# The adaLN sums of the first layer's gate and of the second layer's shift and scale: from beside the gates into slots of the memory stage, by blocks of 128 columns

## The chip, the cores and the metric

The kernel runs on one core of a Trainium2 chip. Its time is the device time of one execution in microseconds; less is better. The engines that matter here are TensorE (PE, with its weight loads, PEld), VectorE (DVE), ScalarE (ACT), GpSimd (POOL) and SyncE (SP), which issues nearly all DMAs. Each engine works through its own instructions in the order in which the program has them, and waits for the others by semaphores.

## The reference, cut to what matters

One inference step of a two-layer diffusion backbone, in fp32: 1024 latent tokens ("sample") and 256 context tokens ("prompt") of width 1024. Layer 0 has two groups of heads from one projection, a windowed attention (A) and a bidirectional mLSTM matrix memory (B, 4 heads of 256 x 256 state, two directions); layer 1 is a latent attention (C). In front of each layer the normed input is scaled and shifted, and behind each the output is gated, by rows that a small product makes from the conditioning (adaLN):

```python
def _adaln(cond, w, b):
    m = jax.nn.silu(cond) @ w + b
    shift, scale, gate = jnp.split(m[:, None, :], 3, axis=-1)
    return shift, scale, gate
...
        sh_p, sc_p, gt_p = _adaln(c_ctx[None, :], w_mod[l], b_mod[l])
        sh_s, sc_s, gt_s = _adaln(c, w_mod[l], b_mod[l])
        hp = _rmsnorm(yp, norm_g[l]) * (1.0 + sc_p) + sh_p
        hs = _rmsnorm(ys, norm_g[l]) * (1.0 + sc_s) + sh_s
        ...
            out_p, (k_ctx, v_ctx, mem, nrm_, mx) = _mixer_ab(hp, *wts, None, None)
        ...
        yp = yp + gt_p * out_p
        ys = ys + gt_s * out_s
```

`w_mod[l]` is 1024 x 3072 in fp32, and there are two conditionings, one of the samples and one of the prompt. The change concerns three of the six 1024-column parts of the two layers: the gate of layer 0, and the shift and scale of layer 1.

## The kernel before, in words

TensorE's time goes to products of fp32 values, each made of three passes over two rounded halves (`wh`, `wl` of the weights, `hTh`, `hTl` of the tokens). The weights of a projection come in blocks of 256 columns (`DenseBlock`): a DMA brings two of the eight row tiles at a time (`wf`), ScalarE rounds each to `wh` (L353), POOL subtracts to get `wl` (L354), TensorE runs the block's units (for each of three chunks of tokens and two halves of columns, 24 matmuls), and a function of the block's own evacuates each unit.

The stages, with their times in the trace of the kernel before: start, norms and first values (0 to 60 us); the block of attention values with the gates' 16 columns (60 to 90.4); four blocks of the memory's head 0, namely queries (QB), keys (KB), values (VB) and output gate (OB), beside the scalar gates of the memory (90.4 to 240); the memory stage (240 to 1098); the attention stage (1098 to 1500); the output projection of layer 0 (1500 to about 1600); layer C (to the end, at 2643).

The adaLN sums are not made on TensorE as a product: `mod_steps` (L284) makes them by blocks of 512 columns. For each of eight row tiles a DMA brings 128 x 512 of `w_mod` (`mw`, 256 KB), and VectorE multiplies it with the conditioning's column (L319 for the first tile) or multiplies and adds (L321) into `macc`, one operation for each of the two conditionings. `total` then sums over the partitions with two fp32 matmuls against a selecting matrix (`sel`, in the trace under the tile name `unit`), takes a bank from `K.ps()`, adds the bias (`bmod`, L306), and stores the row in DRAM (`modd`). Six such blocks, 2 of layer 0's gate and 4 of layer 1's shift and scale, are due here: 96 operations on VectorE, 48 DMAs of `mw`. (The shift and scale of layer 0 are made earlier, the gate of layer 1 later, near 1660 to 1790 us by 256 columns; neither is touched.)

What sets the order before 240 us: `layer_ab` calls `dense.run(1, 1)`, a weave of `gates(...)` with `dense.stream(1, 1)`, and `dense.run(3, 1)`; the stream takes one step of `dense.mods` (two VectorE operations) for every unit of cost that a projection block spends. What is left of the sums is drained, and `mod_cols(K, 1, mp)` fetches layer 1's rows and turns them into columns. A scheduler then places the instructions on each engine. `gates` makes the log gates, transposes them to rows (`LI`, `LF`), scans them along the tokens (`gB` sums, `gM` running maxima, L1328 to L1335), and transposes the results back to columns, `K.cols`: ten transposes of each of three 36-row tiles.

In the memory stage the order is written by hand (`manual_schedule`). `beside_memory` goes through 174 slots: in each, the steps of the visits that are due (a visit is one chunk of 128 tokens, one head, one direction; 80 of them, two slots apart), what earlier slots put off by `K.later`, a share of the units of 24 projection blocks, and `dense.pump`, which asks for weights and splits them. PSUM there has three banks S for the visits, three `mm` for projection units, and two T for transposes.

## Time and profile before

| what | value |
|---|---|
| median of 3 runs | 2644.18 us (2643.71 to 2646.58) |
| profiled execution: its own time | 2644.84 us |
| profiled execution: span | 2643.0 us |
| TensorE busy | 2572.9 us (97%) |
| VectorE busy | 1777.3 us (67%) |
| ScalarE busy | 1406.5 us (53%) |
| POOL busy | 1167.1 us (44%) |
| DMA | 348.79 MB, mean 132 GB/s |

The busy shares are averages over all stages. A wait counts where the engine that waits is the one that sets the stage's end; that is read from the stage. The ends of matmuls are modelled, since they are pipelined: the distance between two starts is the measure of what one takes.

### The profile page before, as it was taken

What the parts mean: (1) busy time and instruction counts of PE and PEld (TensorE: products, weight loads), DVE (VectorE), ACT (ScalarE), POOL (GpSimd) and SP (SyncE); (2) the same over time, 40 slices, a digit from 0 to 9 for tenths busy, and PEclk for the clock granted to TensorE, in tenths of its full rate; (3) what the DMA queues carried; (4) which work ended last, traced back from release to release, by engine and by line L of the source; (5) the groups of instructions that cost most, each with busy time, mean ns of one, the idle gap of its engine ahead of it and who ended that gap; (6) DMA issues with size and microseconds to landing.
All of it is one profiled execution on the core that took longest, in us unless ns stands there. A gap on an engine that the chain in (4) does not pass through costs nothing.

```text
span 2643.0 us, 48201 instructions
## 1 busy us (share of the span) xinstructions
PE 2572.9 (97%) x16209; PEld 2262.3 (86%) x16209; DVE 1777.3 (67%) x4040; ACT 1406.5 (53%) x3598; POOL 1167.1 (44%) x1533
## 2 busy tenths in 40 slices
PE   7989999999999999989999999999899999999998
PEld 6878899898998888868888877987799999999887
DVE  6883565655746666388777545335788888888853
ACT  5222443543533433287666533322788888888842
POOL 4342333423434434275545453223455545555642
PEclk9989999999999999999999999999999999999999
DMA  7554556556657655463433463333311101101333
GB/s 247 181 157 157 161 178 198 175 171 195 199 169 225 213 164 185 140 204 111 136 102 111 130 197 130 121 95 114 104 30 30 44 29 40 35 19 30 122 104 128
DMA packets 344586, 348.79 MB, mean 132 GB/s; under 512 B 29610, under 2 KB 291415, under 8 KB 344083
## 3 DMA queue, kind: packets, MB, share of 16 engines
q1 hardware_dynamic: 344338, 345.71, 42.1%
q8 instruction: 129, 2.11, 0.3%
q14 instruction: 119, 0.97, 0.1%
HBM read 235.09 MB, written 110.51 MB: 131 GB/s over the span
## 4 chain that ended last, share of the span: by engine, by line
PE 81%; DVE 6%; DMA 3%; ACT 3%; issue 3%; POOL 2%; SPq 1%; POOLq 0%; DVEq 0%; ACTq 0%
PE mm L103 34%; PE S L103 27%; PE V L103 8%; PE T L107 6%; PE D L103 3%; PE mm L107 2%; SPq L138 1%; PE T L103 1%; DVE macc L321 1%; DVE att_nm L1109 0%; DVE xT L536 0%; ACT att_p L1114 0%; POOL wl L354 0%; DMA o_x<-y 0%; DMA w<-in_w_out_ab 0%
## 5 line engine op out<-in xcount | busy, mean ns | idle before, releaser
L354 POOL TENSOR_TENSOR wl<-wf,wh 128x256 fp32r<-128x256 f32 (+2 forms) x288 | 250.7, 896 | 448.6 <-ACT wh L353 378.6
L103 PE MATMUL mm<-hTh,wh 128*128 128x512 f32 (+1 forms) x912 | 328.6, 360 | 1.6 <-DVE scr L620 0.9
L103 PE MATMUL mm<-hTl,wh 128*128 128x512 f32 (+1 forms) x912 | 325.5, 357 | 0.0
L103 PE MATMUL mm<-hTh,wl 128*128 128x512 f32 (+1 forms) x912 | 325.4, 357 | 0.0
L103 PE MATMUL S<-cK,cQ 96*128 96x512 f32 (+3 forms) x1248 | 298.3, 364 | 3.3 <-ACT cPb L2154 1.0
L2202 DVE TENSOR_TENSOR cpl<-T,cph 128x512 fp32r<-128x512 f32 x336 | 228.5, 685 | 38.0 <-ACT cph L2201 34.5
L103 PEld LDWEIGHTS S<-cK,cQ 96*128 96x128 f32 (+1 forms) x1248 | 192.8, 189 | 25.9 <-ACT cPb L2154 2.9
L2201 ACT CAST cph<-T 128x512 fp32r<-128x512 f32 x336 | 192.3, 589 | 26.6 <-PE T L107 13.4
L103 PEld LDWEIGHTS mm<-hTh,wl 128*128 128x128 f32 x912 | 172.0, 189 | 26.4
L103 PEld LDWEIGHTS mm<-hTh,wh 128*128 128x128 f32 x912 | 171.9, 188 | 25.7 <-DVE bmod L306 1.7
L103 PEld LDWEIGHTS mm<-hTl,wh 128*128 128x128 f32 x912 | 171.9, 188 | 22.9
L2152 DVE TENSOR_REDUCE cmx<-S 128x1 f32<-128x512 f32 x256 | 172.7, 681 | 16.4 <-PE S L103 15.2
L103 PE MATMUL V<-cph,cV 128*128 128x256 f32 x672 | 177.0, 290 | 1.0 <-DVE co L2217 1.0
L103 PE MATMUL V<-cpl,cV 128*128 128x256 f32 x672 | 171.9, 285 | 1.3 <-DVE cpl L2202 1.3
L103 PE MATMUL S<-w,o_ah 128*128 128x512 f32 x492 | 152.1, 395 | 3.0 <-ACT w L819 1.9
L103 PE MATMUL mm<-w,o_ah 128*128 128x512 f32 x468 | 151.4, 402 | 0.0
L2133 POOL TENSOR_SCALAR cPa<-cPa,cst 128x512 f32<-128x512 f32 x128 | 99.3, 776 | 118.0 <-DVE cst L2130 87.5
L1123 POOL TENSOR_SCALAR att_p<-att_p,att_den 128x640 f32<-128x640 f32 (+1 forms) x128 | 97.5, 774 | 103.4 <-DVE att_den L1120 41.0
L1134 ACT CAST att_ph<-mm 128x512 fp32r<-128x512 f32 x168 | 98.5, 586 | 81.5 <-PE mm L107 80.0
L353 ACT CAST wh<-wf 128x256 fp32r<-128x256 f32 (+2 forms) x288 | 102.0, 409 | 70.1 <-DMA wf<-in_w_in_ab 30.5
L1135 DVE TENSOR_TENSOR att_pl<-mm,att_ph 128x512 fp32r<-128x512 f32 x168 | 115.7, 689 | 32.1 <-ACT att_ph L1134 27.3
L103 PE MATMUL mm<-wh,hTh 128*128 128x256 f32 x480 | 135.8, 283 | 0.0
(432 smaller groups left out, 7823.5 us busy)
## 6 DMA issues: line engine op xcount, KB each, us to landing
wf<-in_w_in_ab SPq DMA_DIRECT2D x120, 256.0 KB
in<-in SPq DMA_DIRECT2D x40, 514.0 KB
in<-in SPq DMA_DIRECT2D x32, 386.0 KB
mw<-in_w_mod SPq DMA_DIRECT2D x48, 256.0 KB
in<-scr SPq DMA_DIRECT2D x40, 258.0 KB
o_x<-y SPq DMA_DIRECT2D x20, 512.0 KB
wm<-in_w_mod SPq DMA_DIRECT2D x16, 512.0 KB
in<-cx SPq DMA_DIRECT2D x32, 256.0 KB
```

The lines of the kernel that those rows point to most:

```text
L103: return self.nc.tensor.matmul(out, lhsT, rhs, start=start, stop=stop)
L107: self.nc.tensor.transpose(out, in_, self.ident[:p, :p])
L138: self.nc.sync.dma_start(f(out), f(in_))
L353: K.nc.scalar.copy(wh, wf[:, k])
L354: K.nc.gpsimd.tensor_sub(wl, wf[:, k], wh.bitcast(F32))
L1123: nc.gpsimd.tensor_scalar(pv, pv, den[:, i:i + 1], 1.0, ALU.mult, ALU.mult)
L1134: K.nc.scalar.copy(ph, self.T)
L1135: K.nc.vector.tensor_sub(pl, self.T, ph.bitcast(F32))
L2133: nc.gpsimd.tensor_scalar(pv, pv, wt[:, c:c + 1], rd, ALU.mult, ALU.mult)
L2152: nc.vector.tensor_reduce(mx[:, b, c:c + 1], S, AX.X, ALU.max, negate=True)
L2201: nc.scalar.copy(ph, T_)
L2202: nc.vector.tensor_sub(pl, T_, ph.bitcast(F32))
```

## The change

The six blocks of 512 columns become 24 of 128. `mod_slots` replaces `mod_steps` for them: a DMA brings two row tiles of 128 columns (128 KB, in pieces of 512 bytes, two buffers), one step makes four VectorE operations of 128 columns (two at L364 and two at L366, or four at L366), and behind the eighth row tile the total's two matmuls, now 128 columns wide, the bias (L352) and the store follow, each put off by a slot. There are 96 steps. They are taken in the loop over slots of the memory stage, in those slots two behind which a block is `light`; a slot adds 4 x 24 / (0.52 x 174) = 1.06 steps when it is. Not light are the attention's query blocks and the memory's query and key blocks; all others are. The total takes its bank from the three `mm` banks.

`mod_cols` for layer 1 moves behind the attention stage, ahead of the loads of the output weights. `K.cols` becomes three tiles of 8 columns a chunk instead of 36, filled by two copies each, and the visits' column numbers follow.

```diff
@@ -331,2 +331,48 @@
 
+def mod_slots(K, p, blocks):
+
+    nc = K.nc
+    parts = [(l, f, k) for l, f in blocks for k in range(0, KD, 2)]
+    asked = []
+
+    def ask():
+        if parts:
+            l, f, k = parts.pop(0)
+            w = K.t(p, [128, 2, 128], F32, "mw", 2)
+            K.dma(w, K.I["w_mod"][l, k * 128:(k + 2) * 128, f:f + 128].rearrange("(k p) f -> p k f", p=128))
+            asked.append(w)
+
+    def total(l, f, acc, bm):
+        ps = K.ps()
+        for cd in range(2):
+            K.mm(ps[0:2, 0:128], K.sel[cd], acc[:, cd], cd == 0, cd == 1)
+        K.later(partial(out, l, f, bm, ps))
+
+    def out(l, f, bm, ps):
+        nc.vector.scalar_tensor_tensor(bm, ps[0:2, 0:128], 0.5, bm, ALU.mult, ALU.add)
+        K.later(lambda: K.dma(K.modd[l][:, f:f + 128], bm))
+
+    for _ in range(2):
+        ask()
+    for l, f in blocks:
+        acc = K.t(p, [128, 2, 128], F32, "macc", 1)
+        for k in range(KD):
+            w = asked[0][:, k % 2, :]
+            for cd in range(2):
+                c = K.condT[:, cd * KD + k:cd * KD + k + 1]
+                if k == 0:
+                    nc.vector.tensor_scalar(acc[:, cd], w, c, None, ALU.mult)
+                else:
+                    nc.vector.scalar_tensor_tensor(acc[:, cd], w, c, acc[:, cd], ALU.mult, ALU.add)
+            if k == KD - 1:
+                bm = K.t(p, [2, 128], F32, "bmod", 1)
+                K.dma(bm, K.I["b_mod"][l:l + 1, f:f + 128].to_broadcast([2, 128]))
+            if k % 2:
+                asked.pop(0)
+                K.later(ask)
+                if k == KD - 1:
+                    K.later(partial(total, l, f, acc, bm))
+                yield True
+
+
 class DenseBlock:
@@ -337,2 +383,3 @@
         self.src, self.w, self.wf, self.when, self.asked = K.I[src][0], [], [], [], 0
+        self.light = True
 
@@ -454,2 +501,3 @@
             b.load()
+            self.light = b.light
             yield from b.run()
@@ -684,3 +732,3 @@
     gt = K.const.tile([128, NT, 16], F32, tag="gt", name="gt")
-    mods = [(0, 2 * D + f) for f in range(0, D, 512)] + [(1, f) for f in range(0, 2 * D, 512)]
+    mods = [(0, 2 * D + f) for f in range(0, D, 128)] + [(1, f) for f in range(0, 2 * D, 128)]
     blocks = [DenseBlock(K, wp, [(O_VA, 256), (O_G, 16)], partial(a_values, K, gt), 6, 272)]
@@ -734,13 +782,7 @@
         blocks += a_proj(K, wp, g)
-    mp = left("mod")
-    dense.mods = mod_steps(K, mp, mods, 4)
     K.tp = gtp = left("gtmp")
-    dense.run(1, 1)
-    weave(gates(K, gp, gtp, gt), 5, dense.stream(1, 1), 10)
-    dense.run(3, 1)
-    for _ in dense.mods:
-        pass
-    mod_cols(K, 1, mp)
+    dense.run(1)
+    weave(gates(K, gp, gtp, gt), 5, dense.stream(1), 10)
+    dense.run(3)
     gtp.release()
-    mp.release()
     K.tp = tp
@@ -770,3 +812,3 @@
         K.pairs = True
-        beside_memory(K, bp, dense, 24, 240)
+        beside_memory(K, bp, dense, 24, 240, mods)
         K.pairs, K.spread = False, True
@@ -782,2 +824,3 @@
     p = left("wo2")
+    mod_cols(K, 1, p)
     wt = load_wout(K, p, w, range(2, 8))
@@ -964,3 +1007,5 @@
     q, z = units(q_done), units(z_done)
-    return [DenseBlock(K, wp, [(o + g * 256, 256)], f, 6, 272) for o, f in ((O_QA, q), (O_ZA, z))]
+    blocks = [DenseBlock(K, wp, [(o + g * 256, 256)], f, 6, 272) for o, f in ((O_QA, q), (O_ZA, z))]
+    blocks[0].light = False
+    return blocks
 
@@ -1385,3 +1430,3 @@
     for nm, src in (("cv", v), ("cws", ws), ("cem", M)):
-        col = pp.tile([128, NT, 36], F32, tag=nm, name=nm)
+        col = pp.tile([128, NT, 8], F32, tag=nm, name=nm)
         ps = K.psT()
@@ -1389,3 +1434,5 @@
             K.tr(ps[:, c * 36:(c + 1) * 36], src[:, c * 128:(c + 1) * 128])
-        nc.vector.tensor_copy(col, ps[:, 0:NT * 36].rearrange("p (c q) -> p c q", q=36))
+        pv = ps[:, 0:NT * 36].rearrange("p (c q) -> p c q", q=36)
+        for a in range(2):
+            nc.vector.tensor_copy(col[:, :, 4 * a:4 * a + 4], pv[:, :, 32 * a:32 * a + 4])
         K.cols.append(col)
@@ -1468,4 +1515,7 @@
 
-    return [DenseBlock(K, wp, [(o + h * 256, 256)], f, 6, 272) for o, f in
-            ((O_QB, partial(qk_block, 0)), (O_KB, partial(qk_block, 1)), (O_VB, by_token(v_split)), (O_OB, by_token(o_tanh)), (O_ZB, z_block))]
+    blocks = [DenseBlock(K, wp, [(o + h * 256, 256)], f, 6, 272) for o, f in
+              ((O_QB, partial(qk_block, 0)), (O_KB, partial(qk_block, 1)), (O_VB, by_token(v_split)), (O_OB, by_token(o_tanh)), (O_ZB, z_block))]
+    for b in blocks[0:2]:
+        b.light = False
+    return blocks
 
@@ -1486,3 +1536,3 @@
         self.c, self.dr, self.sample, self.first, self.other, self.turn = c, dr, sample, first, other, turn
-        self.key, self.col = (dr, sample), 32 * dr + h
+        self.key, self.col = (dr, sample), 4 * dr + h
         self.zero = first and not sample
@@ -1575,3 +1625,3 @@
         for i in range(2):
-            q = 32 * (self.dr if i else 1 - self.dr) + self.h
+            q = 4 * (self.dr if i else 1 - self.dr) + self.h
             nc.scalar.activation(um[:, i, :], um[:, i, :], AF.Exp, bias=K.cols[0][:, c, q:q + 1])
@@ -1730,4 +1780,6 @@
 
-def beside_memory(K, bp, dense, n, total):
+def beside_memory(K, bp, dense, n, total, mods):
+
 
+    steps, light, room = mod_slots(K, bp, mods), [], 0
     vs = [v for h in range(4) for v in visits(K, bp, h)]
@@ -1737,2 +1789,3 @@
     slots = lead + 2 * len(vs) + max(o for o, _ in Visit.STEPS)
+    rate = 4 * len(mods) / (0.52 * slots)
     for s in range(slots):
@@ -1747,2 +1800,8 @@
         dense.pump(s)
+        light.append(dense.light)
+        room += light[max(0, s - 2)] * rate
+        while room >= 1:
+            next(steps, None)
+            room -= 1
+    assert next(steps, None) is None
     flow.drain()
```

In the program's order VectorE's instructions between the gates' scans and the end of `LI` were these in the kernel before (`gM`, `gB` the scans, `macc` the sums, `cx` and `scr` the convolution of the query block, `LF` and `LI` the log gates):

```order
L1335 SCALAR_TENSOR_TENSOR gM<-LF,m_1363,LI 4x1024 x2
L321 SCALAR_TENSOR_TENSOR macc_1631<-mw_1531,condT,macc_1631 128x512
L321 SCALAR_TENSOR_TENSOR macc_1631<-mw_1555,condT,macc_1631 128x512 x2
L1328 SCALAR_TENSOR_TENSOR gB<-rst,LF 4x1280
L1329 SCALAR_TENSOR_TENSOR gB<-rst,LF 4x1280
L1335 SCALAR_TENSOR_TENSOR gM<-LF,LI 4x256 x2
L321 SCALAR_TENSOR_TENSOR macc_1631<-mw_1592,condT,macc_1631 128x512
L1411 COPY scr_1526<-S_1540 128x1
L321 SCALAR_TENSOR_TENSOR macc_1631<-mw_1592,condT,macc_1631 128x512
L1425 SCALAR_TENSOR_TENSOR cx_1582<-scr_1569,cw,cx_1582 128x512
```

and are these after the change, with the four small copies and the two subtractions behind them as before:

```order
L1380 SCALAR_TENSOR_TENSOR gM<-LF,m_1306,LI 4x1024 x2
L1479 SCALAR_TENSOR_TENSOR cx_1280<-scr_1284,cx_1280 128x512
L1472 SCALAR_TENSOR_TENSOR cx_1389<-scr_1385,cw,cx_1389 128x256
L1373 SCALAR_TENSOR_TENSOR gB<-rst,LF 4x1280
L1374 SCALAR_TENSOR_TENSOR gB<-rst,LF 4x1280
L1380 SCALAR_TENSOR_TENSOR gM<-LF,LI 4x256 x2
L1473 SCALAR_TENSOR_TENSOR cx_1389<-scr_1385,cw,cx_1389 128x256
```

Five sums are gone from between the scans; three convolution operations stand where one stood.

On TensorE the transposes of `LI` and its two companions stood in the kernel before between units of the second projection block (`S_1766` is a unit's bank):

```order
L103 MATMUL S_1712<-hTh_131,wl_1235 128x512
L103 MATMUL S_1766<-hTh_133,wh_1202 128x256
L103 MATMUL S_1766<-hTl_134,wh_1202 128x256
L107 MATMUL T_1476<-small,LI 128x36 x10
L103 MATMUL S_1766<-hTh_133,wl_1203 128x256
```

and stand after the change inside the last unit of the first block, whose last matmuls are behind them:

```order
L103 MATMUL S_1513<-hTh_133,wh_771 128x256
L107 MATMUL T_1411<-small,LI 128x36 x10
L103 MATMUL S_1513<-hTl_134,wh_771 128x256
L103 MATMUL S_1513<-hTh_133,wl_772 128x256
L103 MATMUL S_1590<-hTh_129,wh_1162 128x512
```

They moved ahead by 48 matmuls of 512 columns and 4 of 256. Counted from the start of the query block, 144 matmuls of 512 columns and 50 of 256 stood ahead of them, and 96 and 46 do now.

In the memory stage VectorE's order in a block of values looked like this in the kernel before (`scr` the evacuation of a unit, `Cs` the state, `kwl` and `ql` the lower halves of a visit's keys and queries):

```order
L1445 TENSOR_TENSOR scr_4260<-mm_4194,scr_4260 128x256
L1446 CAST scr_4260<-unit 128x2x2
L1645 SCALAR_TENSOR_TENSOR Cs_2884<-Cs_2884,w0b,S_4243 128x258
L1645 SCALAR_TENSOR_TENSOR Cs_2884<-Cs_2884,w0b,S_4244 128x258
L1607 SCALAR_TENSOR_TENSOR kwl_4308<-km_3997,cws,kwh_4307 128x256
```

and after the change there is a step of sums between the evacuations and the state's update:

```order
L1493 CAST scr_4261<-unit 128x2x2
L1492 TENSOR_TENSOR scr_4265<-mm_4197,scr_4265 128x256
L1493 CAST scr_4265<-unit 128x2x2
L366 SCALAR_TENSOR_TENSOR macc_4224<-mw_4167,condT,macc_4224 128x128 x4
L1695 SCALAR_TENSOR_TENSOR Cs_2578<-Cs_2578,w0b,S_4247 128x258
```

On TensorE a total stands between two units of a projection, in the `mm` banks:

```order
L103 MATMUL mm_4097<-wh_3793,hTh_131 128x256
L103 MATMUL mm_4097<-wl_3794,hTh_131 128x256
L103 MATMUL mm_4097<-wh_3793,hTl_132 128x256
L103 MATMUL mm_4169<-macc_2960,unit 2x128 x2
L103 MATMUL mm_4172<-wh_3526,hTh_131 128x256
```

`mm_4169` is the bank that the total takes, behind the unit of `mm_4097` and ahead of that of `mm_4172`.

## Rows read from the trace of the kernel before

**Rows 1.** From the page: the span, and the chain of work that ended last, as shares of the span by engine.

```profile
span 2643.0 us, 48201 instructions
...
PE 81%; DVE 6%; DMA 3%; ACT 3%; issue 3%; POOL 2%; SPq 1%; POOLq 0%; DVEq 0%; ACTq 0%
```

**Rows 2.** Busy time by stage: window, its length, then busy us and instructions of PE, PEld, DVE, ACT and POOL, the granted TensorE clock, the share of the DMA engines' time, and GB/s.

```profile
90.40:141.30 50.90, 44.33 (x220) 34.96 (x221) 47.17 (x90) 13.90 (x34) 25.64 (x21) 0.96 0.42 129
141.30:240.00 98.70, 91.72 (x625) 79.28 (x625) 64.20 (x131) 24.46 (x59) 34.71 (x28) 0.95 0.51 151
240.00:1098.00 858.00, 855.09 (x5510) 772.68 (x5511) 510.39 (x1301) 349.69 (x935) 326.05 (x400) 1.00 0.60 184
...
1500.00:1600.00 100.00, 96.39 (x437) 78.12 (x436) 43.41 (x64) 31.33 (x58) 51.51 (x45) 1.00 0.60 194
```

**Rows 3.** What TensorE waited for between 60 and 240 us: the waiting group, what released it, us in all, times, longest.

```profile
PE T L107 <- DVE LI L1358: 5.6, 1, 5.6
PE S L103 <- POOL wl L354: 3.6, 2, 2.6
PE S L103 <- DVE scr L1445: 2.8, 1, 2.8
PE mm L103 <- DVE bmod L306: 0.8, 1, 0.8
PE S L103 <- ACT scr L1407: 0.6, 1, 0.6
```

**Rows 4.** Busy time between 60 and 240 us of the instructions that touch `macc` alone: PE, PEld and DVE, then clock, DMA share and GB/s of the stretch.

```profile
60.00:240.00 180.00, 11.64 (x24) 1.45 (x24) 67.67 (x96) 0.95 0.51 154
```

**Rows 5.** The tile `macc` by form: min, median and max ns, first and last start, form; the first two lines from 1600 to 1830 us (the gate of layer 1, by 256 columns), the last from 60 to 240 us.

```profile
L321 DVE SCALAR_TENSOR_TENSOR macc<-mw,condT,macc x56: 465/475/1132, 1660.1 to 1794.1; 128x256 f32<-128x256 f32 x56
...
L319 DVE TENSOR_SCALAR macc<-mw,condT x8: 331/341/1022, 1658.9 to 1788.0; 128x256 f32<-128x256 f32 x8
...
L321 DVE SCALAR_TENSOR_TENSOR macc<-mw,condT,macc x84: 730/741/1231, 70.4 to 224.6; 128x512 f32<-128x512 f32 x84
```

**Rows 6.** TensorE's timeline: start us, length us, line, operation, form, count, and in brackets the idle time before it and what ended it. The macc rows are totals.

```profile
90.43 0.50 PE L103 MATMUL S<-hTh,wh 128*128 128x512 f32 x1
...
135.46 0.28 PE L103 MATMUL S<-hTl,wh 128*128 128x256 f32 x1
141.33 1.25 PE L107 MATMUL T<-small,LI 36*128 36x36 f32 x10 [5.59 <-DVE LI L1358]
...
232.25 0.28 PE L103 MATMUL S<-wh,hTl 128*128 128x256 f32 x1
232.45 1.88 PE L103 MATMUL S<-macc,unit 128*2 128x512 f32 x4
234.26 0.39 PE L103 MATMUL S<-wh,hTh 128*128 128x256 f32 x1
234.48 0.28 PE L103 MATMUL S<-wl,hTh 128*128 128x256 f32 x1
234.60 0.28 PE L103 MATMUL S<-wh,hTl 128*128 128x256 f32 x1
...
254.54 0.61 PE L103 MATMUL T<-in 128*128 128x128 f32 x4
254.91 0.48 PE L103 MATMUL mm<-hTh,wh 128*128 128x512 f32 x1
...
1766.55 0.40 PE L103 MATMUL S<-h1Th,wl 128*128 128x512 f32 x1
1766.88 1.02 PE L103 MATMUL S<-macc,unit 128*2 128x256 f32 x4
1767.83 0.50 PE L103 MATMUL S<-h1Th,wh 128*128 128x512 f32 x1
1768.17 0.39 PE L103 MATMUL S<-h1Tl,wh 128*128 128x512 f32 x1
1768.40 0.39 PE L103 MATMUL S<-h1Th,wl 128*128 128x512 f32 x1
```

**Rows 7.** VectorE's timeline between 118 and 142 us, columns as in rows 6.

```profile
118.25 2.33 DVE L1335 TENSOR_TENSOR_SCAN gM<-LF,m,LI 4x1024 f32<-4x1024 f32 x1
...
122.97 3.31 DVE L321 SCALAR_TENSOR_TENSOR macc<-mw,condT,macc 128x512 f32<-128x512 f32 x3
126.20 3.35 DVE L1328 TENSOR_TENSOR_SCAN gB<-rst,LF 4x1280 f32<-4x1280 f32 x1
...
139.18 2.00 DVE L1358 TENSOR_TENSOR LI<-LI,gB 36x1280 f32<-36x1280 f32 x1
```

**Rows 8.** Busy time of three 20 us stretches of the memory stage, columns as in rows 2; the first is in a block of output gates, the other two beside the block of the attention's keys.

```profile
560.00:580.00 20.00, 20.00 (x171) 20.00 (x170) 7.76 (x17) 6.44 (x18) 5.65 (x8) 1.00 0.63 186
...
820.00:840.00 20.00, 20.00 (x117) 17.40 (x116) 16.73 (x41) 6.11 (x17) 10.73 (x11) 1.00 0.71 227
840.00:860.00 20.00, 18.93 (x113) 16.18 (x111) 13.73 (x32) 9.04 (x26) 10.25 (x12) 1.00 0.73 240
```

**Rows 9.** The largest wait of VectorE for TensorE's matmuls in the memory stage: us in all, times, longest.

```profile
DVE Cs L1645 <- PE S L103: 64.0, 29, 5.7
```

**Rows 10.** The splitting of weights on POOL as a group of instructions, the first line between 60 and 240 us, the second between 240 and 960: count, busy us, mean ns of one, and POOL's idle time before them with what ended most of it.

```profile
L354 POOL TENSOR_TENSOR wl<-wf,wh 128x256 fp32r<-128x256 f32 x36 | 48.7, 1379 | 77.3 <-issue 38.1 <-ACT wh L353 34.4 <-PE S L103 4.7
...
L354 POOL TENSOR_TENSOR wl<-wf,wh 128x256 fp32r<-128x256 f32 x160 | 126.5, 816 | 258.8 <-ACT wh L353 233.6 <-PE mm L103 22.5 <-PE S L103 2.7
```

## The prediction

> **What bounds the kernel now.** I read the page first, then the chain of waits, then busy time by stage, then what TensorE waited for in the stage that the change empties, and last single rows of both engines there. The profiled execution took 2644.84 us: a span of 2643.0 and 1.84 around it; the median of the runs, 2644.18, is 0.66 below. The chain is 81% TensorE and 6% VectorE [rows 1], so work on VectorE counts only where TensorE waits for it. By stage [rows 2]: from 90.4 to 240 us (four projection blocks beside the gates and the adaLN sums) TensorE is idle for 6.6 + 7.0 us and its granted clock averages 0.96 and 0.95; in the memory stage (240 to 1098) it is busy 855 of 858 us at clock 1.00, with VectorE at 510 of 858. So the change takes VectorE work out of a stage in which TensorE sometimes waits, and puts it, with TensorE work of its own, into a stage in which TensorE never rests.
>
> **The stage that is emptied.** Between 60 and 240 us the sums are 96 VectorE operations, 67.7 us [rows 4], and six totals on TensorE.
>
> The totals: from the start of the matmul ahead of one (232.25) to that of the one behind (234.26) are 2.01 us, 0.12 of them the former's own, and the first matmul behind takes 0.1 more (0.22) than the next (0.12): 2.0 each [rows 6], six times: 12.0 us off TensorE's queue here, all of it on the path.
>
> The wait for the gates (5.6 us, the longest) [rows 3]: before, TensorE came to the transposes of LI at 135.5 and went on at 141.3 [rows 6]. VectorE's chain from the first scan (118.25) to the end of LI (139.18 + 2.00) is 22.9 us, with five sums in it: 3.2 for three [rows 7] and some 0.7 each for the two others, by the median of 741 ns [rows 5], so 4.6. The new order has no sum there, but three convolution operations in place of one (some 0.9 us more): 19.2. When can it start? The transposes of the forget gates now stand behind 48 matmuls of 512 columns (0.23 each) and 15 of 256 (0.12) from 90.43: 90.4 + 11.0 + 1.8 + 1.1 for the input gates' transposes = 104.3, with ScalarE's copies 106.3. LI is then ready at 125.5. But the order also moves the transposes of LI forward, past 48 matmuls of 512 columns and 4 of 256 (11.5 us): TensorE reaches them 45.0 - 11.5 - 2.0 (a total) - 1.0 (a wait on POOL) = 30.5 us behind 90.43, at 120.9. It waits 4.6 us instead of 5.6. So this wait is not removed: chain and transposes both come some 15 us earlier. Gain 1.0. The ends: all 5.6 gained, or 2 us lost if ScalarE's copies come late.
>
> The other waits, 7.8 us [rows 3]: those on the evacuation (2.8), on the bias (0.8), on ScalarE (0.6) and the smaller one on POOL (1.0) stand behind sums in VectorE's queue, and I take them as gone: 5.2. The longer one on POOL (2.6) is for weights, whose splitting the sums only slow; it stays. The clock of 0.95 over 98.7 us is 4.9 us lost; most follows the wait for the gates, which stays, so 1.3 comes back. The stage gives 12.0 + 1.0 + 5.2 + 1.3 = 19.5 us; bounds 10 (the totals, and 2 us more of waiting) and 30 (12.0 + 5.6 + 7.8 + 4.9).
>
> **What the memory stage gets.** Totals: 24 of 128 columns. No row shows this width. A total of 256 columns takes 1766.55 to 1767.83 = 1.28 less 0.23, plus 0.11 by which the matmul behind it is longer (0.34 for 0.23): 1.16 [rows 6]. The line through 2.0 and 1.16 gives 0.74 at 128. From below: the four fp32 records of 128x128 in the scores take 0.37 (254.54 to 254.91) [rows 6]. From above: 1.16. I take 0.74, since it follows the same instruction down: 24 x 0.74 = 17.8 us (8.9 to 27.8). Nothing hides it, since TensorE has no idle time there [rows 2]: the same columns in four times as many pieces cost 5.8 us more than before.
>
> Sums: 336 multiply-adds and 48 multiplies of 128 columns. By the medians 741 ns at 512 and 475 at 256 [rows 5] a multiply-add is 342 ns at 128; a multiply, 341 at 256, lies between 0.17 and 0.34: 0.25. With 24 biases, taken at 0.28: 115 + 12 + 7 = 134 us, twice the 67.7 before. VectorE goes from 510 to 644 us of 875. The slots that get them are about half: 14 of the stage's 24 blocks count as light, and a slot is 858 / 174 = 4.9 us, so 1.06 steps of four operations add 1.4 us, 28%. In a light stretch (560 to 580) VectorE is busy 7.8 of 20 us [rows 8] and waits for TensorE's products 29 times, 64 us in all [rows 9]: 5.7 us more hide there. Not so where the keys' rotary work runs: the block of keys counts as light, and VectorE has 16.7 of 20 us at 820 and 13.7 at 840, where TensorE already loses 1.1 us [rows 8]. With 5.7 more the first stretch is over-full by 2.4 us, which TensorE sees late: 3 us. Each total also takes one of the three PSUM banks of the projection for over a slot, so the unit behind it must find its bank evacuated one unit earlier; in blocks of 256-column units (24 matmuls of 0.12, 2.8 us) that leaves about 3 us for an evacuation: 1 us in all. So 4 us, from 0 (every sum hidden) to 12 (half a microsecond at each of the 24 totals).
>
> What is queued behind the new waits: on VectorE, which runs in order, a sum whose weights are late holds the next visit's split of the state; the load is asked for two slots (10 us) ahead. On SyncE the load waits until the buffer's last sum is done, and behind it stand the next visit's loads, wanted three slots later: nothing, as long as VectorE is less than a slot late. 96 loads of 128 KB, 24 of biases and 24 stores replace 48 of 256 KB and 12: the same 12.6 MB, 8% of the 158 MB that the stage moves at 184 GB/s with DMA at 0.60 [rows 2]: hidden.
>
> **The columns of the second layer** are made after the attention instead of at 241 us: two DMAs ahead of output weights, one transpose and five small VectorE operations, where TensorE is idle 3.6 of 100 us [rows 2]. What leaves the old place is about as much; 0 to 2 us, I take 0.2. The six narrower copies of the gate columns have no waiter that I can see: 0.
>
> Sum: -19.5 + 17.8 + 4 + 0.2 = +2.5 us on 2644.84, so 2647.3 for such an execution, and 0.66 less for the median: 2646.6. A measurement of this kernel can tell about 0.2% (5.3 us) from no change, and this is within it.
>
> **The rivals.**
> Faster: VectorE's release is worth its upper end. If the gates' chain is done before TensorE arrives, the clock stays up too: stage -27; totals at the lower price of 0.55: 13; waits 2. Together -12: 2632. For it: every wait of rows 3 but one names an engine that the sums delay. Against it: both queues were moved, and by the sum above the order again brings TensorE to LI before VectorE.
>
> Slower: POOL falls behind on the weights. The splits of a block's last four pieces come as the block before ends, and TensorE needs them some 5 us later. Beside the sums of the old stage a split took 1379 ns on the mean, in the memory stage 816, with most as short as ever [rows 10]: some were held up for long. At 1379 four splits are 2.3 us later; with about 1.1 us of cover lost at each of the eleven switches out of light blocks that is 13 us: +15.5, so 2660. It decides from about 1.1 us a split in the memory stage. Against it: POOL is busy only 326 of 858 us there [rows 2], and it is one block in three whose switch is tight.
> The Trainium skill (SBUF — State Buffer, Who interferes with whom) says that a VectorE operation with two SBUF inputs and a GpSimd one that reads SBUF exclude each other for a whole instruction. The sums have two such inputs, so by that rule each can hold a split; rows 10 agree in kind, and the rule would also cap what one sum of 0.34 us holds up at 0.34.
>
> The change doesn't do what it says: the stage at 90 to 240 us ends as late as its weights and gates do, with or without sums. Then it gives the totals alone, 12 us, and the balance is -12 + 17.8 + 4 + 0.2 = +10: 2654. For it: the gates' wait stays by my own working, and the longest wait on POOL too.
>
> **How the numbers follow.** No change to be told, 2646.6 (its own range 2639 to 2649.5): 0.42. Faster, 2632: 0.24. Weights late, 2660: 0.16; only the totals saved, 2654: 0.18. So faster 0.24, same 0.42, slower 0.34. The range of 8 in 10, from the faster rival's centre to the slowest's: 2632 to 2660; it takes in the bounds of the stage (10 to 30) against those of the totals (9 to 28), not both at their ends.
>
> **What would show it.** The first projection matmul of the memory stage starts near 220 us instead of 240; TensorE still waits 3 to 6 us for LI, at about 121; the 128-column totals make the matmul behind them start 0.6 to 0.8 us late; VectorE has some 640 us busy in the memory stage and TensorE's waits there stay under 6 us. Wrong: no wait for LI (then faster), or waits on POOL's splits or on banks (DVE) of more than 12 us in the memory stage, or a total under 0.45 us.

## The result and the profile after

The changed kernel took 2654.95 us (median of 6 runs, 2651.93 to 2655.74) beside 2643.39 (6 runs, 2642.63 to 2646.58) for the kernel before: ratio 1.0039, interval 1.0029 to 1.0049. It is slower by 0.39%, inside the stated range (2632 to 2660), but above the 2639 to 2649.5 of the likeliest case. The profiled execution took 2655.13 us.

The page after, span and chain by engine, answers to [rows 1]: TensorE's share rose from 81 to 83%.

```profile
span 2653.3 us, 48754 instructions
...
PE 83%; DVE 6%; DMA 3%; issue 3%; ACT 2%; POOL 2%; SPq 1%; POOLq 0%; DVEq 0%; ACTq 0%
```

To compare stages of different start, take the first matmul of each. After, the memory stage's first projection matmul and the attention's first `V` matmul are these (TensorE's timeline):

```profile
214.68 0.39 PE L103 MATMUL mm<-hTh,wh 128*128 128x512 f32 x1
...
1128.93 0.48 PE L103 MATMUL V<-att_ph,att_v 128*128 128x512 f32 x1
```

Before, they were these:

```profile
239.95 0.50 PE L103 MATMUL mm<-hTh,wh 128*128 128x512 f32 x1 [0.77 <-DVE bmod L306]
...
1122.09 0.48 PE L103 MATMUL V<-att_ph,att_v 128*128 128x512 f32 x1
```

So the emptied stage became 25.2 us shorter (149.5 to 124.3 from the start of the query block) and the memory stage 32.1 us longer (882.1 to 914.2). The rest is 0.6 us in the attention stage and output projection and 3.4 us in layer C: 10.9 in all, of which 0.5 come back at the two ends of the span (2653.3 for 2643.0). By stage, columns as in [rows 2], first the two stages after the change, then the memory stage before it:

```profile
90.40:214.60 124.20, 120.81 (x820) 110.42 (x820) 63.39 (x142) 37.45 (x89) 41.72 (x45) 0.97 0.35 102
214.60:1128.90 914.30, 900.23 (x5759) 801.99 (x5758) 640.01 (x1727) 356.39 (x955) 334.71 (x407) 0.99 0.63 190
```

```profile
239.95:1122.09 882.14, 879.23 (x5663) 793.69 (x5663) 520.39 (x1324) 357.90 (x954) 330.34 (x406) 1.00 0.59 183
```

TensorE, which idled 2.9 us in the memory stage before, idles 14 there, and VectorE is busy for 640 us where it was busy for 520. What TensorE waited for between 200 and 1110 us (columns as in [rows 3]), and then the one wait left between 60 and 240 in TensorE's timeline:

```profile
PE T L107 <- DVE hh L1739: 5.5, 1, 5.5
PE mm L103 <- DVE bmod L352: 4.0, 2, 2.6
PE mm L103 <- DVE scr L693: 1.6, 2, 1.2
PE mm L103 <- DVE macc L366: 0.9, 1, 0.9
...
PE mm L103 <- POOL wl L401: 0.5, 2, 0.3
```

```profile
124.21 1.25 PE L107 MATMUL T<-small,LI 36*128 36x36 f32 x10 [3.39 <-DVE scr L1456]
```

All four large ones name VectorE; POOL's splits are where they were before (0.5). The name of a releaser can mislead: in the last row it is a small operation, but the transposes read `LI`, which VectorE ended at 124.06 (VectorE's timeline):

```profile
122.59 1.47 DVE L1403 TENSOR_TENSOR LI<-LI,gB 36x1280 f32<-36x1280 f32 x1
```

The longest wait, beside the block of the attention's keys, costs more than its length (TensorE's timeline):

```profile
847.68 0.69 PE L107 MATMUL T<-small,scr 128*128 128x128 f32 x2 [5.48 <-DVE hh L1739]
848.02 0.78 PE L103 MATMUL mm<-hTh,wh 128*128 128x512 f32 x1
848.59 0.63 PE L103 MATMUL mm<-hTl,wh 128*128 128x512 f32 x1
849.02 0.63 PE L103 MATMUL mm<-hTh,wl 128*128 128x512 f32 x1
...
851.36 0.39 PE L103 MATMUL mm<-hTh,wl 128*128 128x512 f32 x1
851.59 0.40 PE L103 MATMUL mm<-hTh,wh 128*128 128x512 f32 x1
```

Behind it a matmul of 512 columns takes 0.43 us from start to start, and 0.23 three microseconds on: the lower of the two clock levels (1.2 and 2.4 GHz), then the higher. The granted clock says the same, here and behind the longer of the two waits for the bias (columns as in [rows 2]):

```profile
622.86:625.86 3.00, 3.00 (x7) 2.42 (x8) 2.89 (x10) 0.15 (x1) 1.93 (x2) 0.51 1.05 322
847.68:851.36 3.68, 3.68 (x10) 2.98 (x11) 2.79 (x6) 2.77 (x9) 0.97 (x2) 0.54 0.13 38
```

At a clock of 1.00 these two stretches would have taken 1.5 and 2.0 us, by their clock, so some 1.5 and 1.7 us were lost.

VectorE's side, as groups between 205 and 1100 us (count, busy us, mean ns, idle before):

```profile
L366 DVE SCALAR_TENSOR_TENSOR macc<-mw,condT,macc 128x128 f32<-128x128 f32 x336 | 132.7, 452 | 9.7 <-DMA mw<-in_w_mod 9.5
...
L364 DVE TENSOR_SCALAR macc<-mw,condT 128x128 f32<-128x128 f32 x48 | 16.2, 379 | 58.0 <-DMA mw<-in_w_mod 30.4 <-PE mm L103 27.5
```

A sum takes 452 ns on the mean, not 342, and ten times (27.5 us) a block's first multiply stood waiting for a total of the block before, since there is one buffer for the sums; VectorE runs in order, so all behind it waited too. (The 30.4 us are one wait that ends at 217.6, and no wait of TensorE stands behind it.) Seven times, 9.5 us in all, VectorE stood for weights of the sums that had not landed. One of TensorE's two waits for the bias stands behind the longest of these (VectorE's timeline, then TensorE's):

```profile
367.31 0.88 DVE L366 SCALAR_TENSOR_TENSOR macc<-mw,condT,macc 128x128 f32<-128x128 f32 x3 [3.99 <-DMA mw<-in_w_mod]
```

```profile
369.64 0.38 PE L103 MATMUL mm<-wh,hTh 128*128 128x256 f32 x1 [1.41 <-DVE bmod L352]
```

### The profile page after: what moved, and what is told of

It is laid out like the page before. It is cut to its first block, busy times and chain, and to the rows that moved or that the text cites. A ratio compares the mean times of both kernels' runs of the same rounds, so it can differ in the third digit from the quotient of the medians.

```text
span 2653.3 us, 48754 instructions
## 1 busy us (share of the span) xinstructions
PE 2581.8 (97%) x16281; PEld 2267.8 (85%) x16281; DVE 1838.4 (69%) x4349; ACT 1405.9 (53%) x3598; POOL 1157.0 (44%) x1533
## 4 chain that ended last, share of the span: by engine, by line
PE 83%; DVE 6%; DMA 3%; issue 3%; ACT 2%; POOL 2%; SPq 1%; POOLq 0%; DVEq 0%; ACTq 0%
PE mm L103 33%; PE S L103 30%; PE V L103 8%; PE T L107 6%; PE D L103 3%; PE mm L107 2%; SPq L138 1%; DMA mw<-in_w_mod 1%; PE T L103 1%; DVE macc L366 0%; DMA o_x<-in_x_sample 0%; DMA wk<-in_w_kvb_c 0%; POOL w L863 0%; DVE xT L584 0%; POOL wl L401 0%
## 5 line engine op out<-in xcount | busy, mean ns | idle before, releaser
L401 POOL TENSOR_TENSOR wl<-wf,wh 128x256 fp32r<-128x256 f32 (+2 forms) x288 | 235.9, 845 | 432.4 <-ACT wh L400 390.5
L366 DVE SCALAR_TENSOR_TENSOR macc<-mw,condT,macc 128x128 f32<-128x128 f32 x336 | 132.7, 452 | 9.7 <-DMA mw<-in_w_mod 9.5
```

What stands on the lines that cost most here:

```text
L366: nc.vector.scalar_tensor_tensor(acc[:, cd], w, c, acc[:, cd], ALU.mult, ALU.add)
L401: K.nc.gpsimd.tensor_sub(wl, wf[:, k], wh.bitcast(F32))
```

## The experiments

The table gives each run's median, the ratio to the kernel before on the same chip, the stages in us cut at the same matmuls as above, in the profiled execution, and TensorE's idle time in the memory stage.

| run | median us | ratio, interval | start | gates | memory | attention | layer C | idle |
|---|---|---|---|---|---|---|---|---|
| before | 2643.39 | 1 | 90.4 | 149.5 | 882.1 | 486.2 | 1026.2 | 2.9 |
| after | 2654.95 | 1.0039, 1.0029 to 1.0049 | 90.4 | 124.3 | 914.2 | 486.8 | 1029.6 | 13.9 |
| e1 no sums | 2638.93 | 0.9974, 0.9965 to 0.9984 | 90.6 | 124.2 | 899.1 | 485.3 | 1030.1 | 3.3 |
| e2 no totals | 2633.01 | 0.9958, 0.9942 to 0.9975 | 93.0 | 124.0 | 892.2 | 484.8 | 1028.9 | 9.9 |
| e3 none | 2619.31 | 0.9908, 0.9893 to 0.9923 | 88.2 | 123.8 | 881.5 | 486.5 | 1029.0 | 2.7 |
| e4 two accumulators | 2652.45 | 1.0027, 1.0016 to 1.0038 | 93.4 | 124.1 | 911.8 | 485.1 | 1028.2 | 11.6 |
| e5 keys not light | 2653.61 | 1.0028, 1.0017 to 1.0039 | 91.3 | 124.4 | 912.4 | 486.3 | 1029.5 | 11.5 |
| e6 256 columns | 2637.93 | 0.9972, 0.9961 to 0.9983 | 88.4 | 124.1 | 897.4 | 487.0 | 1033.2 | 3.2 |
| e7 = e5 + e6 | 2633.10 | 0.9948, 0.9933 to 0.9962 | 88.2 | 122.9 | 895.6 | 485.6 | 1028.8 | 2.8 |
| e8 late columns alone | 2647.14 | 1.0007, 0.9997 to 1.0017 | 88.7 | 152.9 | 882.3 | 487.5 | 1025.6 | 3.5 |
| e9 half steps | 2655.55 | 1.0042, 1.0027 to 1.0057 | 93.0 | 124.0 | 911.1 | 485.2 | 1034.0 | 10.8 |
| e10 256, double steps | 2637.10 | 0.9973, 0.9963 to 0.9983 | 89.0 | 124.0 | 899.8 | 486.2 | 1028.7 | 5.2 |
| e11 aside of splits | 2653.19 | 1.0036, 1.0022 to 1.0049 | 92.7 | 124.3 | 912.4 | 486.0 | 1029.3 | 12.2 |
| e12 = e2 + e5 | 2629.35 | 0.994, 0.9923 to 0.9956 | 93.3 | 124.0 | 888.2 | 487.4 | 1027.2 | 6.0 |

The start varies by 5 us among these executions; no run was made on why, so effects are read from the stage concerned.

**The bill by parts: e1, e2, e3.** What is left out is in each expectation; e1 and e2 in short:

```diff
-                if k == 0:
+                if k == 0 and first:
                     nc.vector.tensor_scalar(acc[:, cd], w, c, None, ALU.mult)
-                else:
-                    nc.vector.scalar_tensor_tensor(acc[:, cd], w, c, acc[:, cd], ALU.mult, ALU.add)
```

```diff
-        ps = K.ps()
-        for cd in range(2):
-            K.mm(ps[0:2, 0:128], K.sel[cd], acc[:, cd], cd == 0, cd == 1)
-        K.later(partial(out, l, f, bm, ps))
+        out(l, f, bm, acc)
```

> Leaves out the multiply-adds of all 24 blocks but the very first two multiplies (the rows of shift, scale and gate are then not the reference's); loads, totals, biases and stores stay where the change puts them. Theory A (the bill by parts): the memory stage is 32 us longer than before because of the totals (24 x 0.65 = 15.7 us), VectorE coming late (11 us of new waits of TensorE) and the clock behind these waits (3 us). Without the sums the waits and the clock go and the totals stay: 14 us off, 2641 (2638 to 2645). Theory B (the 96 loads and 48 small DMAs, and SyncE's queue, make it): nothing goes, 2652 to 2656. Theory C (the totals' hold on the mm banks makes the waits): little goes, 2648 to 2652.

> Leaves out the totals' two matmuls and their bank; the sums, loads, biases and stores stay, and the bias operation reads the first row of the sums (two bias buffers, asked for earlier), so the rows are not the reference's. Theory A: the totals' 15.7 us go, and of the waits those for the bias and the sums (about 5 us) and VectorE's holds behind a total: 2634 (2630 to 2639). Theory B: the totals alone, 2639 to 2642. Theory C: totals and nearly all waits, 28 us: 2625 to 2629.

> Leaves out the 24 blocks altogether, loads and totals too (the rows are the bias alone). Theory A, B and C alike: the memory stage falls back to its 882 us and the gain of the emptied stage (25.3 us) stands alone: 2622 to 2627, if the 3.4 us that layer C was longer in the profile stay, 2619 to 2622 if they go with the sums. It sets the bottom from which e1 and e2 are read: if the totals are worth what A says, e1 is 15 to 17 us above it.

By the memory stage: without either 881.5; totals alone 17.6 more (0.73 each, idle time as good as unchanged); sums alone 10.7 more; both 32.7, which is 4.4 above their sum. So the totals cost what they were forecast to. The rest, 15.1, is VectorE's lateness: all but 1 us of it is TensorE's new idle time (13.9 for 2.7) and, by the two stretches at half clock above, some 3 us of clock. The large waits all name VectorE. Theory A holds for its parts, and e1 and e2 came out in its ranges. B falls as a price of the loads and stores themselves, since e1 keeps them all and idles 3.3 us; loads that come late for their sum, as the one at 367, can't be seen in e1, which has no sums. C falls too: without totals most of the waiting stays (9.9 us), above all this one (TensorE's waits in e2, 210 to 1130 us):

```profile
PE T L107 <- DVE hh L1739: 6.0, 1, 6.0
```

e3's time, 2619.3, is that of the case in which layer C's lengthening goes too, but its profile doesn't bear that out: layer C is 2.8 us longer than before, and the start 2.2 us shorter.

**One buffer or two: e4.**

```diff
-        acc = K.t(p, [128, 2, 128], F32, "macc", 1)
+        acc = K.t(p, [128, 2, 128], F32, "macc", 2)
```

> Two buffers for the sums instead of one (the room comes from the gates' tile, which goes from a constant to a buffer that is released); the order of every engine stays. Theory A says that VectorE's ten waits for a total (27.5 us, because the next block's first multiply needs the one buffer that the total still reads) make it late: they vanish, and of TensorE's 13.9 us of waits those at 617 to 623 with their clock (5.4 us) and part of the others: 2647 to 2651. Rival D: VectorE is late because of the work itself, above all beside POOL's splits, where four sums take up to 3.1 us instead of 1.1; the waits go elsewhere and the time stays, 2653 to 2656.

The holds behind totals are gone from VectorE's waits, and the stage is 2.4 us shorter, 911.8. That is about half of the 4.4 and far less than the 27.5 us that VectorE stood: most of that standing it made up, while its waits for weights of the sums rose from 9.5 to 18.7 us. The wait beside the keys stayed (5.5 us). The time lies between the two ranges; rival D has more right than theory A.

**Where the sums may stand: e5, e12, e11.**

```diff
     blocks.append(DenseBlock(K, wp, [(O_KA, 256)], partial(a_keys, K), 6, 272))
+    blocks[-1].light = False
...
-    rate = 4 * len(mods) / (0.52 * slots)
+    rate = 4 * len(mods) / (0.48 * slots)
```

> The block of the attention's keys no longer counts as light, and the rate is raised (0.48 for 0.52) so that the 96 steps still end. Theory A': of the sums' 10.7 us (what they cost alone in the memory stage, without totals), the wait of 5.5 to 6.0 us for the visit's last operation beside the block of keys, and the half clock behind it (2 us), are one place, where VectorE has too much: they go, and the denser steps elsewhere cost 1: 2647 to 2650. Rival D': the over-full stretch only moves to the next rich block, 2652 to 2656.

> e2 and e5 together: sums without totals (left out as in e2), and none beside the block of the attention's keys. Alone the sums cost 10.7 us in the memory stage (892.2 against 881.5), 6.0 of them one wait beside the keys with 2 us of half clock behind it. Theory J: that place is nearly all of it, and the rest of the sums hides as the prediction said: the stage falls to 883 to 885, the time from 2633 to 2624 to 2627; that e5 gained only 1.8 us is then because with totals in the mm banks the next place (4.2 us at an evacuation) is just behind. Theory K: VectorE is too full in several places, and the wait moves on without totals too: 889 to 892, 2630 to 2634.

In e5 the 5.5 us beside the keys have become 1.9 (the second row), and 4.2 have come at an evacuation ahead of them, with half clock (0.50) behind (TensorE's waits, 210 to 1120 us):

```profile
PE mm L103 <- DVE scr L693: 4.2, 1, 4.2
PE mm L103 <- DVE scr L649: 1.9, 1, 1.9
```

The stage gained 1.8 us, and the time is in the rival's range. But neither of these waits is an over-full stretch that moved. Ahead of each, VectorE stood for the one buffer of the sums (VectorE's timeline, ScalarE's, VectorE's again):

```profile
781.02 0.48 DVE L364 TENSOR_SCALAR macc<-mw,condT 128x128 f32<-128x128 f32 x2 [6.75 <-PE mm L103]
```

```profile
783.00 0.42 ACT L1719 ACTIVATE tho<-hh 128x256 f32<-128x256 f32 x1 [11.40 <-DVE hh L1717]
```

```profile
784.42 1.28 DVE L693 SCALAR_TENSOR_TENSOR scr<-scr,mm 128x512 f32<-128x512 f32 x2 [1.45 <-ACT scr L692]
...
820.54 0.48 DVE L364 TENSOR_SCALAR macc<-mw,condT 128x128 f32<-128x128 f32 x2 [4.52 <-PE mm L103]
```

The first multiply of a block waited 6.75 us for the total of the block before, which stood behind other matmuls in TensorE's queue; ScalarE waited for the `hh` behind that multiply, the evacuation (L692, then L693) came late, and TensorE stood 4.2 us for its bank, to 785.16. The 4.5 us at 820.5 stand ahead of the 1.9, and VectorE works without a pause between them. So e5 with a second buffer (e4 and e5 together) is the rival that was left untested. Without totals, and so without such holds, the step gained 4.0 (892.2 to 888.2), which lies between theories J and K: the keys are the largest of the sums' places, not nearly all of them.

e11 takes at most one step in a slot and, unless three are due, none in a slot that splits weights:

```diff
-        while room >= 1:
+        while room >= (3 if split else 1) and taken < 1:
```

> The change with at most one step in a slot, and none in a slot in which a weight tile is split unless three are due. In the change's trace the 27 steps of four operations without POOL work beside them take 1.13 to 1.14 us each, the 40 with it 1.96 on the mean and up to 3.14, since sum and split take turns. Theory H (the sums are held by POOL, and that is what makes VectorE late): the mean operation falls from 452 towards 360 ns, the waits from 13.9 to 6 or 8 us, the time to 2646 to 2650. Rival: the holds fall, the waits move to the slots that now have the steps (not light ones too), 2652 to 2656.

The holds hardly fell (group of VectorE in e11):

```profile
L366 DVE SCALAR_TENSOR_TENSOR macc<-mw,condT,macc 128x128 f32<-128x128 f32 x336 | 130.6, 445 | 11.0 <-DMA mw<-in_w_mod 10.9
```

So the edit did not do what it was to do: by a count of its trace, of 69 steps of four sums 40 still had POOL's work beside them, above all splits. Theory H is neither shown nor refuted as to the time.

**How much, or how long at a time: e6, e9, e10, and e7.** e6 makes 12 blocks of 256 columns, with a load and a step per row tile; the room comes from two planes of masks that leave the constants. e9 keeps 128 columns and halves the step; e10 doubles e6's step:

```diff
-    parts = [(l, f, k) for l, f in blocks for k in range(0, KD, 2)]
+    parts = [(l, f, k) for l, f in blocks for k in range(KD)]
...
-            w = K.t(p, [128, 2, 128], F32, "mw", 2)
+            w = K.t(p, [128, 256], F32, "mw", 2)
...
-        acc = K.t(p, [128, 2, 128], F32, "macc", 1)
+        acc = K.t(p, [128, 2, 256], F32, "macc", 1)
```

> 12 blocks of 256 columns, a load and a step per row tile (two operations of 256), one buffer for the sums as in the change; the room comes from two mask planes that leave the constants. Theory A': the totals cost 12 x 1.16 = 13.9 instead of the 17.6 that e1 over e3 shows, and VectorE's sums some 91 us instead of 134, so that its waits cost 8 to 10 instead of 15: 2655 - 3.7 - 6 = 2645 (2642 to 2649). Rival: what the sums cost is set by the places at which they stand (behind a bank, beside the keys), not by their length: 2650 to 2653.

> 128 columns as in the change, with the same 384 operations, 24 totals and 96 loads, but a step is one row tile (two operations, 0.57 us alone) in place of two (four operations, 1.13 us alone, up to 3.1 us beside POOL's splits), one step ahead of a slot's evacuations and one at its end, and a block's first step never ahead of the former block's total. Theory F (what counts is how long VectorE is away at a time: the evacuations and state updates behind a step come late by its length): TensorE's waits in the memory stage fall from 13.9 to 4 or 5 us, the stage to 902 (881.5 + 17.6 + 3), the time to 2641 to 2645. Theory G (what counts is VectorE's work in all and the number of totals): the stage stays at 910 to 914, 2651 to 2655.

> e6 with its steps taken two at a time in every other due slot: the same operations, loads and 12 totals, but VectorE is away for four operations of 256 columns, 1.9 us alone and up to 3.5 us beside POOL. Theory F: TensorE's waits rise from 3.2 us to about those of the change (10 to 14), the stage from 897 to 906 to 910, the time from 2638 to 2647 to 2651. Theory G: as e6, 2637 to 2641.

In e6 the memory stage is 897.4, 15.9 above none: the 13.9 of twelve totals by [rows 6] and 2 for all else. Halving the step gave 3.1 us in the stage (e9: 911.1, idle 10.8), where theory F wanted 12, and the time not at all; doubling it cost 2.4 (e10: 899.8, idle 5.2), where F wanted 9 to 13. Both stages are as G says: what counts is VectorE's work in all and the number of totals. But neither edit changed the step's length alone. In e9 VectorE stood 40.4 us for weights of the sums (70.9 in its row below, less a first wait of 30.5 as in the change), where the change has 9.5; in e10 its holds for the one buffer, 16.9 us in e6, are gone. So F is not borne out, and not refuted either:

```profile
L366 DVE SCALAR_TENSOR_TENSOR macc<-mw,condT,macc 128x128 f32<-128x128 f32 x330 | 131.4, 439 | 70.9 <-DMA mw<-in_w_mod 70.9
```

VectorE's groups in e6 (205 to 1100 us) come to 108.8 us, where the change has 148.9:

```profile
L369 DVE SCALAR_TENSOR_TENSOR macc<-mw,condT,macc 128x256 f32<-128x256 f32 x168 | 99.2, 631 | 18.4 <-DMA mw<-in_w_mod 18.4
L367 DVE TENSOR_SCALAR macc<-mw,condT 128x256 f32<-128x256 f32 x24 | 9.6, 441 | 47.6 <-DMA mw<-in_w_mod 30.7 <-PE mm L103 16.9
```

Which weighs more was not separated: 40 us less of sums (29 less of VectorE's busy time in the stage, 610.7 for 640.0), 12 banks fewer, or five holds for the buffer instead of ten.

> e5 and e6 together. Theory A': both gains, 2655 - 3.7 - 6 - 6 = 2639 (2636 to 2643), which would be a little faster than before. Rival: as e6 or as e5 alone, 2645 to 2650.

e7 is the fastest of the kernels that leave nothing out: 2633.10 us, 0.52% below the kernel before, 6 us under what was expected. Only 1.8 us of what it is below e6 stand in the memory stage (895.6 for 897.4); the rest is in stages that the edit doesn't touch. The memory stage idles 2.8 us, as much as before the change (212 to 1108 us):

```profile
212.00:1108.00 896.00, 893.11 (x5714) 796.92 (x5713) 611.87 (x1525) 356.89 (x956) 337.48 (x406) 1.00 0.64 194
```

**The moved columns: e8.**

```diff
-    mod_cols(K, 1, mp)
...
+    mod_cols(K, 1, p)
```

> The kernel before with one part of the change alone: the second layer's columns are made after the attention stage instead of at 241 us. Layer C's first part (from its first matmul to its first score) took 267.3 us before, and 269.2 to 271.5 in the change and the four runs so far. If the late columns cause this, it is 269 to 272 here and the time 2646 to 2648 beside a before of 2644; if not, 267 and 2643.5 to 2645.

No difference that can be told (interval 0.9997 to 1.0017), and layer C's first part took 267.9. So the late columns by themselves are not what makes layer C longer. (Its stage beside the gates was 3.4 us longer in this one profile, 152.9; no run was made on why.)

## Why the prediction was right, and where not

**The emptied stage: right in kind, too low.** Forecast -19.5, measured -25.2. The totals went (12.0). TensorE was forecast to reach the transposes of `LI` at 120.9 and to wait 4.6; it reached them at 120.8 (124.21 less 3.39) and waited 3.4, so the gain is 2.2 for 1.0. All the other waits went, the two on POOL's weights too, which the prediction had kept in part: 7.8 for 5.2. The remaining 3.2 are put down to the clock, of which 1.3 had been counted; by the granted clock the stage lost 2.0 and 4.9 us before [rows 2] and 3.7 after (0.97 over 124.2), which is 3.2 less.

**The totals: right.** Forecast 17.8 (0.74 each, from the line through 512 and 256 columns), measured 17.6 by e1 and e3. Single totals of the change's trace say the same (TensorE's timeline):

```profile
401.92 0.28 PE L103 MATMUL S<-in,kwl 128*128 128x258 f32 x1
402.13 0.60 PE L103 MATMUL mm<-macc,unit 128*2 128x128 f32 x4
402.66 0.50 PE L103 MATMUL mm<-hTh,wh 128*128 128x512 f32 x1
402.99 0.40 PE L103 MATMUL mm<-hTl,wh 128*128 128x512 f32 x1
```

From 401.92 to 402.66 are 0.74, less 0.12 of the former's own, plus the 0.1 by which the matmul behind is longer (0.33 for some 0.23): 0.72. Together with the stage's gain this alone would have made the change faster.

**"So 4 us, from 0 to 12": the step that failed.** It was the price of VectorE's lateness in the memory stage, and it measured 15.1 (10.7 with sums alone, 4.4 more with totals). The pieces of it:

- The sums were taken at 342 ns; on the mean they took 452, so they and the multiplies came to 148.9 us, where 127 had been set down. The trace shows why: of the 65 steps of four operations that stand alone, by a count of the trace, the 24 with no POOL work beside them took 1.12 to 1.14 us each, the 41 with POOL work 1.94 on the mean and up to 3.14 (ten of them no longer than without). One with (VectorE, then POOL beside it) and one without:

```profile
335.31 3.14 DVE L366 SCALAR_TENSOR_TENSOR macc<-mw,condT,macc 128x128 f32<-128x128 f32 x4
...
340.31 1.13 DVE L366 SCALAR_TENSOR_TENSOR macc<-mw,condT,macc 128x128 f32<-128x128 f32 x4
```

```profile
334.63 1.43 POOL L401 TENSOR_TENSOR wl<-wf,wh 128x256 fp32r<-128x256 f32 x2 [8.94 <-ACT wh L400]
336.02 0.79 POOL L1605 TENSOR_TENSOR qw<-in,wi 128x256 f32<-128x256 f32 x1
336.77 1.52 POOL L401 TENSOR_TENSOR wl<-wf,wh 128x256 fp32r<-128x256 f32 x2
```

  A sum of 0.28 and a POOL operation of 0.75 take turns. The prediction had looked at this pair from one side only (rows 10: POOL held by sums) and had not asked what POOL does to the sums. But the load that it forecast for VectorE was not too low: 644 us, measured 640. VectorE's other operations in the stage became shorter, such as this one (before, then after), so that its busy time rose by 120 us (520 to 640) and not by the 134 of the forecast:

```profile
L1666 DVE SCALAR_TENSOR_TENSOR hh<-tho,hh 128x256 f32<-128x256 f32 x40 | 29.4, 735 | 0.0
```

```profile
L1716 DVE SCALAR_TENSOR_TENSOR hh<-tho,hh 128x256 f32<-128x256 f32 x40 | 24.4, 610 | 0.0
```

  It reads two operands from SBUF, as the sums do. That POOL's splits, as many as before, now hold sums where they held such operations is argued from these rows, not shown. So what failed is not the load in all, but what a late VectorE costs TensorE.
- The keys' stretch was forecast to be over-full by 2.4 us and to cost 3. It cost a wait of 5.5 to 6.0, and some 1.7 more of half clock, which had not been counted at all.
- The banks were put at 1 us. The waits for the bias and for the last sum are 4.9, and the single buffer for the sums, on which the prediction had said nothing, holds VectorE 27.5 us; a second one gives 2.4 back.
- Late weights of a sum were put at nothing, "as long as VectorE is less than a slot late"; the 4.0 us at 367 ended in 1.4 us of waiting for the bias.

**The moved columns** cost nothing that can be told, as forecast (0.2).

**Layer C, not foreseen.** 3.4 us in the profile. In all runs with the change's code its first part took 269.2 to 275.2 us, in e3 too, where no sum is left; before and in e8 267.3 and 267.9. Waits of 0.6 to 2.6 us in all that name `sz_th` stand there in the change and in all runs with its code, and 0.3 before and in e8; they don't follow the lengths (0.6 in e2, with 270.9 us; 1.8 in e3, with 269.7). Each is one profiled execution, and the cause stays open.

**The rivals.** "Only the totals saved" gave the right time, 2654, for a wrong reason: the stage gave back 25 us, not 12, and the memory stage took 32, not 22. "Faster" had the stage right (27), the totals too cheap (13) and the waits wrong (2). "Weights late" fell: waits on POOL's splits are 0.5 us as before. The pair it named is in conflict, but in the memory stage it is the sums that lose: a split took 820 ns on the mean between 240 and 1090 us before and 836 after.

**The signs, and some luck.** The wait for `LI`, the price of a total and VectorE's busy time came out as the prediction said; the memory stage began at 214.7 instead of 220. Its waits, under 6 us by the forecast, were 13.9, with 7.4 of them on `mm` banks, under the 12 that were to mean wrong. That the range held is in part luck, since two misses ran against each other: the emptied stage gave 5.7 us more than forecast, lateness took 11.1 more, and layer C 3.4 that no term held. With the stage's gain as forecast the time would have been 2660.6, just outside.

The Trainium skill (SBUF — State Buffer, Who interferes with whom) says of a VectorE operation with at most one SBUF input, outside the 2-port modes, that it does not contend with GpSimd, and of one with two that it contends with a GpSimd instruction that reads SBUF. The trace agrees on both. The rows give min, median and max ns in the memory stage. The first two operations read one operand from PSUM and never stretch (30 of the 112 at L1695, by a count of the trace, ran beside a POOL operation of 256 columns). The last two read both from SBUF and reach twice and three times their median.

```profile
L1695 DVE SCALAR_TENSOR_TENSOR Cs<-Cs,w0b,S x112: 465/476/485, 248.6 to 1043.1; 128x258 f32<-128x258 f32 x112
```

```profile
L1711 DVE SCALAR_TENSOR_TENSOR hh<-S,hr,ho x40: 483/484/489, 352.0 to 1060.4; 128x256 f32<-128x256 f32 x40
L1716 DVE SCALAR_TENSOR_TENSOR hh<-tho,hh x40: 404/418/968, 355.0 to 1063.7; 128x256 f32<-128x256 f32 x40
```

```profile
L366 DVE SCALAR_TENSOR_TENSOR macc<-mw,condT,macc x336: 329/346/1037, 218.0 to 983.9; 128x128 f32<-128x128 f32 x168
```

## What to carry to other kernels

Work that is moved beside a busy TensorE is paid in pieces: count the pieces first (24 totals cost 17.6 us where six wider ones had cost 12), and then the time of the filler where it will stand, beside the engines that work there, not where it stood. A mean that is well above the median is a conflict to be priced from both sides, and by the engine's busy time in all, since what one operation loses another may gain. When a stage is tight in several places, emptying one lets another come forward (in e5 the one buffer for the sums), while less work in all, in fewer pieces (e6), took the waits back to 3.2 us; a little room freed in SBUF, for wider pieces, was worth more here than any choice of slots.

## What was not expected of the hardware

Steps of four sums take 1.12 to 1.14 us, all 24 of them, without POOL work beside them, and anything from that to 3.14 with it. VectorE's other operations became shorter when the sums came (`hh` at L1716 from 735 to 610 ns on the mean). And a second buffer that removed all ten holds of VectorE (27.5 us) was worth 2.4 us.
